# Turned squares go through HBM: one transfer out and four back in place of sixteen inside SBUF

## The chip, the cores and the metric

The kernel runs on one core of a Trainium2 chip. A core has five engines that run their own instruction queues side by side: TensorE (matmuls; PE in the profile, and PEld for its weight loads), VectorE (DVE), ScalarE (ACT), GpSimd (POOL) and SyncE (SP), which here only issues transfers. Sixteen DMA engines move data between HBM and the on-chip memory SBUF, which has 128 partitions; matmul results stand in PSUM. The metric is the device time of one execution in microseconds (us), the median of several runs.

## The reference

One decoder layer for 256 tokens of width 2048, in float32:

- `h = RMSNorm(x)`, `z = h @ w_in`, a projection to 7176 columns, split among the heads.
- Four mLSTM heads of 256 channels: `s = (q k^T)` weighted by an exponential of gates, then `s @ v`, divided by a stabilised sum, RMS-normalised per head, times the sigmoid of an output gate.
- Eight attention heads of 128 channels with normalised q and k and a cumulative log-forget bias in a causal softmax.
- `x = x + concat(heads) @ w_out`.
- `u = RMSNorm(x) @ w_up`, halves `a` and `g` of 5632 columns; `a` goes through a causal depthwise convolution of width 3; `x = x + (gelu(a) * g) @ w_down`.
- `x = x + sigmoid(RMSNorm(x) @ w_ple_gate) * (p @ w_ple_proj)`.

## The kernel before

**Matmuls in three products.** Every weight block of 128 x 1024 numbers is loaded by SP as `raw`; ScalarE writes its rounded copy `hi` and VectorE the rest `lo = raw - hi` (L273 and L275 in the first half, L1001 and L1003 in the second). The activations are split the same way. TensorE then adds three products: activation-hi by weight-hi, activation-hi by weight-lo, activation-lo by weight-hi (L304 to L306, L1292 to L1294, L1053 to L1055). A 512-wide matmul starts every 0.227 us; a block of 12 takes 2.72 us.

**Order of the work.** `run_stream` goes through the blocks of `w_in` and `w_out`, `run_units` through the units of `w_up`, `w_down` and the last gate. Loads run ahead by the free `raw` buffers, splits by three to six blocks (`AHEAD_SPLIT`, `PARTS`, `PARTS2`). Work beside the matmuls is hooked on: in the first half generators in `side`, two steps pulled per block; in the second half jobs hung on units by `with_after`, and put behind named splits by `between` (`tc.issue_after`). A planner then fixes each engine's queue before anything runs, from modelled times (`schedule_with_timeline_sim=True`), and adds the waits. On the chip each queue runs in that order.

**Mixed units.** Each group `up_group(q)` but the first carries four units that multiply two of its channel blocks with seven products in place of eight. They need sums of weight blocks on VectorE (`T`, L1325 to L1327) and are split from `xs`. `up_group(q)` has 16 or 18 units and takes 42.8 us; there are 11. Their weights are in `w_up`, then `down` runs twice over the columns of `w_down`, also with such mixed units.

**Turned squares.** Results come with tokens in the partitions; the next matmul wants channels in the partitions. Where TensorE does not transpose, this is done in two steps. `square` (L184, VectorE) transposes 32 x 32 blocks in place, each inside its 32 partitions. `move` then carries the blocks to the right 32 partitions: for each of four source partition groups `a` and four destination groups `b` one transfer from SBUF to SBUF, all issued by POOL (L190):

```
for a in range(4):
    for b in range(4):
        pool.dma_start(out=c[32 * b : 32 * b + 32, a::4], in_=y[32 * a : 32 * a + 32, :, b])
```

There are 25 moves. Four carry the pairs of q and k heads (`qk_squares`, from `qky` to `qkz`), four mLSTM q and k (`qk_group`, from `my` in the tile `spare` to `mqT` or `mk`), one the first two gated mLSTM heads (`mlstm_gate`, `hay` to `haz`), three the new x (`resid`, `x2y` to `x2z`), two x before the last gate (`x3_squares`): 512 KB each. The eleven of the up projection (`up_turn`, from `Y` to `EZ`) carry 1 MB each.

**Who reads them.** `column` takes 32 columns of each moved block, scales them into `hi` on ScalarE (L201) and `lo` on VectorE (L202); `columns` waits until seven blocks have been traced since the move (`since(7, ...)`). `fox_heads` copies q and k on ScalarE (L532), `mk_columns` mLSTM k (L593), and TensorE reads `mqT` directly through `feature` (L641, L644). In the up projection `up_act(q)` runs while group q + 1 is multiplied, from its ninth-last unit on: `first` copies half `a` on ScalarE (L901), four `conv` steps follow (L906, L909), and `last` applies GELU (L915), multiplies by half `g` on VectorE (L916) and splits the result (L140, L141). For some channel pairs `left_sums` then stores sums of it to HBM, also from POOL (L873).

**POOL's other work.** Broadcasts of gate rows (L515), reciprocal roots for the norms (L165), and these stores. They stand in one queue with the moves.

Of the kernel before, what the change touches and what calls it, by code (L numbers as in the profile page):

```python
# [49 lines left out]
def layer_kernel(  # L50
# [7 lines left out]
    act, dve, pe, pool = nc.scalar, nc.vector, nc.tensor, nc.gpsimd  # L58
# [7 lines left out]
    mp = mixers.enter_context(tc.tile_pool(name="mix", bufs=1))  # L66
    kp = ctx.enter_context(tc.tile_pool(name="kept", bufs=1, space=bass.MemoryType.DRAM))
# [7 lines left out]
    def f32(ap):  # L75
        return ap.bitcast(F32)
# [98 lines left out]

    def squares(name):

        return mp.tile([P, NT, 4, 128], F32, tag="sq", name=name)

    def square(y, t, k, src):  # L180

        n = src.shape[1] // P
        o = y[:, t, :, 32 * k : 32 * (k + n)].rearrange("p b (k j) -> p k b j", j=32)
        dve.transpose(o, src)  # L184

    def move(y, c):

        for a in range(4):
            for b in range(4):
                pool.dma_start(out=c[32 * b : 32 * b + 32, a::4], in_=y[32 * a : 32 * a + 32, :, b])  # L190

    def gather(y, name):
        c = mp.tile([P, NT * 4, 128], F32, tag="col", name=name)
        move(y, c)
        return c, done[0]

    def column(c, k, dst, gain):

        src = c[:, :, 32 * k : 32 * k + 32]
        hi, lo = (dst[:, o : o + 256].rearrange("p (a j) -> p a j", j=32) for o in (0, 256))  # L200
        act.activation(hi, src, AF.Copy, scale=gain)  # L201
        dve.scalar_tensor_tensor(out=lo, in0=src, scalar=gain, in1=f32(hi), op0=ALU.mult, op1=ALU.subtract)  # L202

    def columns(yz, dst, k0, gain):

# [137 lines left out]
    with mixers:  # L343
# [19 lines left out]
        my = spare[:, 1024:2048].rearrange("p (t b c) -> p t b c", t=NT, b=4)  # L363
        ssq1 = sm.tile([P, NT, 8], F32, name="ssq1")
        r1 = {}

# [152 lines left out]
        def fox_heads():  # L519
            zv = z["fv"]  # L520

            def gen(heads):
# [3 lines left out]
                for h in heads:  # L526
                    while h // 2 not in qkz or not since(7, qkz[h // 2][1]):
                        yield
                    w = qkz[h // 2][0].rearrange("p a (c h j) -> p h c a j", c=2, h=2)[:, h % 2]
                    qk = mp.tile([P, 512], F32, tag="qk", name="qk", bufs=2)  # L530
                    for c, g_ in ((0, g_fq), (1, g_fk)):
                        act.activation(qk[:, c * 256 : (c + 1) * 256].rearrange("p (a j) -> p a j", j=32),  # L532
                                       w[:, c], AF.Copy, scale=g_)
                    taken.add(h)
                    if h ^ 1 in taken and h // 2 + 1 < FH // 2:
# [46 lines left out]
            side.append(gen(range(1, FH, 2)))  # L582


        mqT = mp.tile([P, 2, NT * 4, P], F32, name="mqT")
        mkT = mp.tile([P, 8, S], F32, name="mkT")

        mk_in = set()
# [1 line left out]
        def mk_columns(grp, start):  # L590
            while not since(7, start):
                yield
            act.copy(mkT[:, 4 * grp : 4 * grp + 4].rearrange("p k (a j) -> p k a j", j=32),  # L593
                     z["mk"][:, grp].rearrange("p a (k j) -> p k a j", j=32))
            mk_in.add(grp)
            yield

        def qk_group(name, grp):
            def f(t, b):
                act.activation(mz[:, t], b, AF.Copy, scale=r1["t"][:, t : t + 1])  # L600
                square(my, t, 0, mz[:, t])
                if t < NT - 1:
                    return
                if name == "mq":
                    move(my, mqT[:, grp])
                    return
                if grp == 0:
                    z["mk"] = zbuf("mk").rearrange("p t c -> p (t c)")[:, 0:2048].rearrange("p (g a c) -> p g a c", g=2, c=P)
                move(my, z["mk"][:, grp])
                side.append(mk_columns(grp, done[0]))  # L610
            return f

        def feature(m, k, t0, t1):

            return m[:, k // 4, 4 * t0 : 4 * t1, 32 * (k % 4) : 32 * (k % 4) + 32]

        WT = {}

# [191 lines left out]
    with tc.tile_pool(name="ffn", bufs=1) as fp:  # L810
# [61 lines left out]
            sums_of(u, f, t)  # L872
            pool.dma_start(out=sums[SEVEN.index(p_)], in_=f32(t).rearrange("p i c -> p (i c)"))  # L873

        Z = EZ.rearrange("p t (a c) -> p (t a) c", c=256)
        a_ = Y[:, 0:BLK].rearrange("p (k s) -> p k s", k=4)
        c_ = Y[:, BLK : 2 * BLK].rearrange("p (k s) -> p k s", k=4)

        def runs(v):
            return v.rearrange("p a (k r) -> p k a r", r=32)  # L880

        def by_run(v):
            return v.rearrange("p k (a r) -> p k a r", r=32)

        def up_rows(t, n, b):

# [1 line left out]

        def up_turn(q):

            y = Y.rearrange("p (t b c) -> p t b c", t=NT, b=4)
            for t in range(NT):
                if q > 0:
                    dve.tensor_add(EZ[:, t], EZ[:, t], xs[:, 1, t * BLK : (t + 1) * BLK])
                square(y, t, 0, EZ[:, t])
            move(y, Z)

        def up_act(q):

            def first():  # L900
                act.copy(by_run(a_), runs(Z[:, :, 0:128]))  # L901
# [12 lines left out]
            def last():  # L914
                act.activation(c_, c_, AF.Gelu)  # L915
                dve.tensor_mul(by_run(c_), by_run(c_), runs(Z[:, :, 128:256]))  # L916
# [256 lines left out]
        def x3_squares(i):  # L1173
            def f(*_):
                if i == 0:
                    x3s["t"] = fp.tile([P, 2, 2, 1024], F32, tag="uB", name="x3s")
                y, z_ = x3s["t"][:, i, 0], x3s["t"][:, i, 1].rearrange("p (a c) -> p a c", c=P)
                y = y.rearrange("p (t b c) -> p t b c", t=NT, b=4)
# [280 lines left out]
```

## Time and profile before

| | us |
|---|---|
| median of 3 runs (1241.19 to 1241.99) | 1241.44 |
| the profiled execution | 1241.07 |
| its span, first to last instruction | 1239.1 |
| TensorE busy | 1232.5 |
| VectorE busy | 901.0 |
| ScalarE busy | 720.9 |
| POOL busy | 244.2 |

The granted TensorE clock is 1.00 throughout. DMA queues moved 276.35 MB, 223 GB/s on average; the queue of POOL's transfers (software_dynamic) 25.50 MB of it, in 7.2% of the time of 16 engines.

How to read the rows: a timeline row gives the start, the duration, engine, code line, operation, out<-in, and in brackets the idle time before and what ended it. `x9` means nine merged neighbours. A group row gives the busy total and the mean in ns. A waits row gives who waited for whom, the total, the number of times and the longest. A row of transfers gives engine, count, KB each and the median us from issue to landing. A row of a stretch gives for PE, PEld, DVE, ACT and POOL the busy time and the count, then the clock, the DMA engines' busy share and GB/s. Tile names are the program's; `hi`, `lo`, `w` are split weights (`w` the two extra buffers of the late part).

### The profile page before, as it was taken

The numbers are of one execution on the slowest core, as the hardware profiler recorded it, in microseconds if no ns is written. First come the engines' busy times: TensorE is split into PE (matmuls) and PEld (weight loads), VectorE is DVE, ScalarE is ACT, GpSimd is POOL, SyncE is SP. The second block draws the span as 40 slices with busy tenths as digits, with TensorE's granted clock in tenths as the row PEclk, the third lists the DMA queues.
The fourth block names the chain that finished last, engine by engine and source line by source line (L and its number), as shares of the span: only waits on it lengthen the run. The fifth ranks groups of instructions, "written<-read, shape, count | busy, mean of one in ns | idle before, by whom it ended". The sixth has DMA issues, their size and how long they took to land.

```text
span 1239.1 us, 16191 instructions
## 1 busy us (share of the span) xinstructions
PE 1232.5 (99%) x5638; PEld 1039.3 (84%) x5638; DVE 901.0 (73%) x1125; ACT 720.9 (58%) x1000; POOL 244.2 (20%) x457
## 2 busy tenths in 40 slices
PE   9999999999999999999999999999999999999998
PEld 7999988888888888888888888888888888888887
DVE  5455566665565665888888898888778998998653
ACT  7565455554554454766676576657645555566542
POOL 2001256513304202022202211220220000050000
PEclk9999999999999999999999999999999999999999
DMA  8766877766557797776877777676895996777560
GB/s 242 207 187 185 233 215 220 207 194 177 173 187 223 217 340 219 223 227 217 260 236 212 224 254 243 192 237 193 257 294 171 316 359 204 264 236 251 179 211 34
DMA packets 134370, 276.35 MB, mean 223 GB/s; under 512 B 15065, under 2 KB 30033, under 8 KB 134161
## 3 DMA queue, kind: packets, MB, share of 16 engines
q1 hardware_dynamic: 118864, 249.66, 64.3%
q0 software_dynamic: 15040, 25.50, 7.2%
q8 instruction: 44, 0.72, 0.2%
q14 instruction: 37, 0.30, 0.1%
q10 hardware_dynamic: 385, 0.16, 0.0%
HBM read 247.46 MB, written 8.93 MB: 207 GB/s over the span
## 4 chain that ended last, share of the span: by engine, by line
PE 99%; DMA 0%; SPq 0%; DVE 0%; ACT 0%; issue 0%; DVEq 0%
PE tg L304 13%; PE tg L305 13%; PE tg L306 13%; PE up L1292 12%; PE up L1294 12%; PE up L1293 12%; PE dnP L1054 1%; PE dnP L1055 1%; PE dnP L1053 1%; PE upP L1292 1%; PE upP L1294 1%; PE upP L1293 1%; PE dn(0, 1)_7885 L1055 1%; PE dn(0, 0)_7881 L1054 1%; PE dn(0, 1)_7885 L1054 1%; PE dn(1, 0)_7889 L1054 1%
## 5 line engine op out<-in xcount | busy, mean ns | idle before, releaser
L275 DVE TENSOR_TENSOR lo<-raw,hi 128x1024 fp32r<-128x1024 f32 (+3 forms) x153 | 177.7, 1162 | 154.8 <-ACT hi L273 154.4
L1294 PE MATMUL up<-hi,x2T 128*128 128x512 f32 x644 | 250.7, 389 | 0.0
L1293 PE MATMUL up<-lo,x2T 128*128 128x512 f32 x644 | 250.6, 389 | 0.0
L273 ACT CAST hi<-raw 128x1024 fp32r<-128x1024 f32 (+3 forms) x153 | 153.1, 1001 | 155.3 <-PE tg L306 122.7
L1292 PE MATMUL up<-hi,x2T 128*128 128x512 f32 x644 | 221.3, 389 | 0.0
L305 PE MATMUL tg<-lo,hT 128*128 128x512 f32 (+2 forms) x480 | 181.5, 379 | 0.0
L304 PE MATMUL tg<-hi,hT 128*128 128x512 f32 (+2 forms) x480 | 180.9, 382 | 0.0
L306 PE MATMUL tg<-hi,hT 128*128 128x512 f32 (+2 forms) x480 | 180.3, 377 | 0.0
L1003 DVE TENSOR_TENSOR lo<-raw,hi 128x1024 fp32r<-128x1024 f32 (+1 forms) x118 | 137.2, 1171 | 43.4 <-ACT hi L1001 42.8
L1001 ACT CAST hi<-raw 128x1024 fp32r<-128x1024 f32 (+1 forms) x118 | 118.8, 1014 | 81.6 <-PE up L1294 35.9
L1294 PEld LDWEIGHTS up<-hi,x2T 128*128 128x128 f32 x644 | 120.9, 188 | 25.1
L1293 PEld LDWEIGHTS up<-lo,x2T 128*128 128x128 f32 x644 | 120.9, 188 | 25.0
L1292 PEld LDWEIGHTS up<-hi,x2T 128*128 128x128 f32 x644 | 120.9, 188 | 25.0
L190 POOL DMA_DIRECT2D EZ<-Y x176 | 93.1, 536 | 122.7 <-DVE Y L184 52.1
L306 PEld LDWEIGHTS tg<-hi,hT 128*128 128x128 f32 x480 | 90.1, 188 | 12.5
L305 PEld LDWEIGHTS tg<-lo,hT 128*128 128x128 f32 x480 | 90.2, 188 | 11.7 <-DVE lo L275 0.3
L304 PEld LDWEIGHTS tg<-hi,hT 128*128 128x128 f32 x480 | 89.7, 188 | 11.7
L1001 ACT CAST hi<-xs 128x1024 fp32r<-128x1024 f32 (+1 forms) x43 | 40.8, 952 | 71.1 <-PE up L1294 50.0
L1003 DVE TENSOR_TENSOR lo<-xs,hi 128x1024 fp32r<-128x1024 f32 (+1 forms) x43 | 47.1, 1098 | 34.7 <-ACT hi L1001 34.7
L873 POOL DMA_DIRECT2D sums<-Sp x9 | 5.2, 575 | 272.3 <-DVE Sp L866 272.3
L1003 DVE TENSOR_TENSOR lo<-u36r,hi 128x1024 fp32r<-128x1024 f32 x36 | 43.6, 1215 | 11.8 <-ACT hi L1001 10.3
L1001 ACT CAST w<-raw 128x1024 fp32r<-128x1024 f32 x27 | 28.4, 1053 | 38.3 <-DVE raw L1102 27.1
(695 smaller groups left out, 2351.9 us busy)
## 6 DMA issues: line engine op xcount, KB each, us to landing
raw<-in_w_in_dram SPq DMA_DIRECT2D x71, 512.0 KB, 4.2
raw<-in_w_up_dram SPq DMA_DIRECT2D x68, 512.0 KB, 5.2
raw<-in_w_down_dram SPq DMA_DIRECT2D x43, 512.0 KB, 6.0
u36r<-in_w_up_dram SPq DMA_DIRECT2D x36, 512.0 KB, 5.0
raw<-in_w_in_dram SPq DMA_DIRECT2D x40, 432.0 KB, 3.8
raw<-in_w_out_dram SPq DMA_DIRECT2D x32, 512.0 KB, 4.7
u32r<-in_w_up_dram SPq DMA_DIRECT2D x31, 512.0 KB, 5.2
EZ<-Y POOLq DMA_DIRECT2D x176, 64.0 KB, 4.6
```

Source lines behind the costliest of these rows:

```text
L190: pool.dma_start(out=c[32 * b : 32 * b + 32, a::4], in_=y[32 * a : 32 * a + 32, :, b])
L273: act.copy(hi, raw[:, :w])
L275: dve.tensor_sub(lo, raw[:, :w], f32(hi))
L304: pe.matmul(o, ah, hi[:, i, :], start=first, stop=False)
L305: pe.matmul(o, ah, lo[:, i, :], start=False, stop=False)
L306: pe.matmul(o, al, hi[:, i, :], start=False, stop=last)
L1001: act.copy(hi, raw)
L1003: dve.tensor_sub(lo, raw, f32(hi))
L1054: pe.matmul(o, ah, lo, start=False, stop=False)
L1292: pe.matmul(o, ah, hi, start=start, stop=False)
L1293: pe.matmul(o, ah, lo, start=False, stop=False)
L1294: pe.matmul(o, al, hi, start=False, stop=stop)
```

## The change

`move` now writes the whole square tile to a scratch tile in HBM (`hop`, two buffers of each width) in one transfer, and reads it back in four, one for each destination group of 32 partitions; all five are issued by POOL. The reads wait for the write. To make the runs contiguous (1 KB or 2 KB for a read, 4 KB or 8 KB for the write) the order of dimensions inside a square changes: destination block first, then token half `t`, and in the moved tile source group `a` before `t`. So every reader walks `t` and `a` in another order. Two VectorE operations are cut in halves by `t`: `lo` in `column`, and the product with half `g` in `last`.

```diff
     def squares(name):
-        return mp.tile([P, NT, 4, 128], F32, tag="sq", name=name)
+        return mp.tile([P, 4, NT, 128], F32, tag="sq", name=name)

     def square(y, t, k, src):
...
-        o = y[:, t, :, 32 * k : 32 * (k + n)].rearrange("p b (k j) -> p k b j", j=32)
+        o = y[:, :, t, 32 * k : 32 * (k + n)].rearrange("p b (k j) -> p k b j", j=32)
         dve.transpose(o, src)

     def move(y, c):
-        for a in range(4):
-            for b in range(4):
-                pool.dma_start(out=c[32 * b : 32 * b + 32, a::4], in_=y[32 * a : 32 * a + 32, :, b])
+        w = y.shape[3]
+        hop = kp.tile([P, 4, NT, w], F32, tag=f"hop{w}", name=f"hop{w}", bufs=2)
+        pool.dma_start(out=hop, in_=y)
+        v = hop.rearrange("(a p) b t c -> p a b (t c)", a=4)
+        for b in range(4):
+            pool.dma_start(out=c[32 * b : 32 * b + 32].rearrange("p a t c -> p a (t c)"), in_=v[:, :, b])
+
+    def tokens(v):
+        return v.rearrange("p a t j -> p t a j")
...
     def column(c, k, dst, gain):
-        src = c[:, :, 32 * k : 32 * k + 32]
-        hi, lo = (dst[:, o : o + 256].rearrange("p (a j) -> p a j", j=32) for o in (0, 256))
+        src = tokens(c[:, :, :, 32 * k : 32 * k + 32])
+        hi, lo = (dst[:, o : o + 256].rearrange("p (t a j) -> p t a j", t=NT, j=32) for o in (0, 256))
         act.activation(hi, src, AF.Copy, scale=gain)
-        dve.scalar_tensor_tensor(out=lo, in0=src, scalar=gain, in1=f32(hi), op0=ALU.mult, op1=ALU.subtract)
+        for t in range(NT):
+            dve.scalar_tensor_tensor(out=lo[:, t], in0=src[:, t], scalar=gain, in1=f32(hi[:, t]),
+                                     op0=ALU.mult, op1=ALU.subtract)
...
         def feature(m, k, t0, t1):
-            return m[:, k // 4, 4 * t0 : 4 * t1, 32 * (k % 4) : 32 * (k % 4) + 32]
+            return tokens(m[:, k // 4, :, t0:t1, 32 * (k % 4) : 32 * (k % 4) + 32])
...
             def first():
-                act.copy(by_run(a_), runs(Z[:, :, 0:128]))
+                act.copy(by_run(a_), runs(Z[..., 0:128]))
...
                 act.activation(c_, c_, AF.Gelu)
-                dve.tensor_mul(by_run(c_), by_run(c_), runs(Z[:, :, 128:256]))
+                for t in range(NT):
+                    v = by_run(c_)[:, :, t]
+                    dve.tensor_mul(v, v, runs(Z[..., 128:256])[:, :, t])
```

The rest of the diff adapts the shapes of `my`, `mqT`, `z["mk"]`, `Z`, `Y` and the x3 tiles, and the readers in `fox_heads` and `mk_columns`, to this order.

More of the change, by code (lines that the diff above doesn't have):

```diff
@@ L362, in layer_kernel @@
         mz = spare[:, 0:1024].rearrange("p (t c) -> p t c", t=NT)
-        my = spare[:, 1024:2048].rearrange("p (t b c) -> p t b c", t=NT, b=4)
+        my = spare[:, 1024:2048].rearrange("p (b t c) -> p b t c", t=NT, b=4)
         ssq1 = sm.tile([P, NT, 8], F32, name="ssq1")
@@ L582, in fox_heads @@
             side.append(gen(range(1, FH, 2)))
-        mqT = mp.tile([P, 2, NT * 4, P], F32, name="mqT")
+        mqT = mp.tile([P, 2, 4, NT, P], F32, name="mqT")
         mkT = mp.tile([P, 8, S], F32, name="mkT")
@@ L592, in mk_columns @@
                 yield
-            act.copy(mkT[:, 4 * grp : 4 * grp + 4].rearrange("p k (a j) -> p k a j", j=32),
-                     z["mk"][:, grp].rearrange("p a (k j) -> p k a j", j=32))
+            act.copy(mkT[:, 4 * grp : 4 * grp + 4].rearrange("p k (t a j) -> p k t a j", t=NT, j=32),
+                     z["mk"][:, grp].rearrange("p a t (k j) -> p k t a j", j=32))
             mk_in.add(grp)
@@ L607, in f @@
                 if grp == 0:
-                    z["mk"] = zbuf("mk").rearrange("p t c -> p (t c)")[:, 0:2048].rearrange("p (g a c) -> p g a c", g=2, c=P)
+                    z["mk"] = zbuf("mk").rearrange("p t c -> p (t c)")[:, 0:2048].rearrange("p (g a t c) -> p g a t c", g=2, t=NT, c=P)
                 move(my, z["mk"][:, grp])
@@ L873, in left_sums @@
             pool.dma_start(out=sums[SEVEN.index(p_)], in_=f32(t).rearrange("p i c -> p (i c)"))
-        Z = EZ.rearrange("p t (a c) -> p (t a) c", c=256)
+        Z = EZ.rearrange("p t c -> p (t c)").rearrange("p (a t c) -> p a t c", t=NT, c=256)
         a_ = Y[:, 0:BLK].rearrange("p (k s) -> p k s", k=4)
@@ L879, in runs @@
         def runs(v):
-            return v.rearrange("p a (k r) -> p k a r", r=32)
+            return v.rearrange("p a t (k r) -> p k t a r", r=32)
         def by_run(v):
-            return v.rearrange("p k (a r) -> p k a r", r=32)
+            return v.rearrange("p k (t a r) -> p k t a r", t=NT, r=32)
         def up_rows(t, n, b):
@@ L889, in up_turn @@
         def up_turn(q):
-            y = Y.rearrange("p (t b c) -> p t b c", t=NT, b=4)
+            y = Y.rearrange("p (b t c) -> p b t c", t=NT, b=4)
             for t in range(NT):
@@ L1176, in f @@
                     x3s["t"] = fp.tile([P, 2, 2, 1024], F32, tag="uB", name="x3s")
-                y, z_ = x3s["t"][:, i, 0], x3s["t"][:, i, 1].rearrange("p (a c) -> p a c", c=P)
-                y = y.rearrange("p (t b c) -> p t b c", t=NT, b=4)
+                y, z_ = x3s["t"][:, i, 0], x3s["t"][:, i, 1].rearrange("p (a t c) -> p a t c", t=NT, c=P)
+                y = y.rearrange("p (b t c) -> p b t c", t=NT, b=4)
                 for t in range(NT):
```

6 lines of the change are left out of this document (3 added, 3 removed).

## The prediction

> **What bounds the kernel now.** I read the page's busy times and chain first, then the waits of the two TensorE rows, then a timeline of each hand-over that the change touches.
>
> ```profile
> span 1239.1 us, 16191 instructions
> PE 1232.5 (99%) x5638; PEld 1039.3 (84%) x5638; DVE 901.0 (73%) x1125; ACT 720.9 (58%) x1000; POOL 244.2 (20%) x457
> PE 99%; DMA 0%; SPq 0%; DVE 0%; ACT 0%; issue 0%; DVEq 0%
> ```
>
> The chain that ended last is TensorE throughout. A busy TensorE could still be a waiting one, so the waits decide.
>
> ```profile
> PE warm L93 <- DVE ones L89: 1.1, 1, 1.1
> PE xT L152 <- DMA xs<-in_x_dram: 1.0, 1, 1.0
> PEld tg L305 <- DVE lo L275: 0.3, 1, 0.3
> ```
>
> These are waits of the first microseconds; none names a turned square. So TensorE is the bound, nothing the moves could release is on its path, and the change can matter only by making TensorE wait. What protects it is the lead: ScalarE's `hi` and VectorE's `lo` of a weight block are ready some microseconds before TensorE reads them. The n-th split belongs to the n-th unit of the written order, so I paired them over the kernel (1,798 `lo` products, as the code has). After the 30 us of start-up the smallest leads are these. First, the mixed units of the up projection, in the second and the eighth of its eleven groups (`up_group` 1 and 7; 1 to 7 all lie between 1.74 and 1.76 us).
>
> ```profile
> 494.18 1.23 DVE L1003 TENSOR_TENSOR lo<-xs,hi 128x1024 fp32r<-128x1024 f32 x1 [1.20 <-ACT hi L1001]
> 497.15 0.39 PE L1293 MATMUL up<-lo,S_up 128*128 128x512 f32 x1
> 751.22 1.22 DVE L1003 TENSOR_TENSOR lo<-xs,hi 128x1024 fp32r<-128x1024 f32 x1 [1.19 <-ACT hi L1001]
> 754.19 0.39 PE L1293 MATMUL up<-lo,S_up 128*128 128x512 f32 x1
> ```
>
> VectorE ends at 495.41 and TensorE reads at 497.15: 1.74 us. Second, the start of the down projection, where loads are late.
>
> ```profile
> 905.00:932.00 27.00, 27.00 (x121) 22.36 (x120) 15.20 (x15) 9.85 (x13) 9.09 (x17) 1.00 0.90 281
> 932.45 1.05 ACT L1001 CAST hi<-raw 128x1024 fp32r<-128x1024 f32 x1 [8.94 <-DMA raw<-in_w_down_dram]
> 933.53 1.23 DVE L1003 TENSOR_TENSOR lo<-raw,hi 128x1024 fp32r<-128x1024 f32 x1 [8.77 <-ACT hi L1001]
> 937.79 0.39 PE L1054 MATMUL dn(0, 0)_7881<-lo,uA 128*128 128x512 f32 x1
> 974.47 1.22 DVE L1003 TENSOR_TENSOR w<-raw,w 128x1024 fp32r<-128x1024 f32 x1
> 978.14 0.39 PE L1054 MATMUL dn(1, 0)_7889<-lo,uC 128*128 128x512 f32 x1
> ```
>
> From 905 to 932 us the DMA engines are 90% busy, ScalarE waits 8.94 us for a load, and the lead is 937.79 - 934.76 = 3.03 us; at 978.14 it is 2.45.
>
> **The move itself.** There are 25 moves: 4 of query-key pairs, 4 of mLSTM q and k, 1 of the gated heads, 3 of x2, 11 of the up projection, 2 of x3. Each loses 16 POOL transfers and gets 5. I take the up projection's, twice as large as the others.
>
> ```profile
> 526.25 4.73 POOL L190 DMA_DIRECT2D EZ<-Y  x9 [36.77 <-ACT hi L1001]
> 535.67 2.24 POOL L190 DMA_DIRECT2D EZ<-Y  x4 [1.64 <-DMA EZ<-Y]
> 546.42 1.03 ACT L901 COPY Y<-EZ 128x1024 f32<-128x1024 f32 x1
> 548.43 1.23 DVE L1003 TENSOR_TENSOR lo<-u36r,hi 128x1024 fp32r<-128x1024 f32 x1 [2.18 <-ACT hi L1001]
> 554.27 0.39 PE L1293 MATMUL up<-lo,x2T 128*128 128x512 f32 x1
> EZ<-Y POOLq DMA_DIRECT2D x176, 64.0 KB, 4.6
> sums<-Sp POOLq DMA_DIRECT2D x9, 512.0 KB, 4.8
> kept_x<-xs SPq DMA_DIRECT2D x1, 2048.0 KB, 9.3
> xs<-in_w_up_dram SPq DMA_DIRECT2D x20, 256.0 KB, 5.4
> rowF<-keptF POOLq DMA_DIRECT2D x8, 128.0 KB, 4.2
> L873 POOL DMA_DIRECT2D sums<-Sp x9 | 5.2, 575 | 272.3 <-DVE Sp L866 272.3
> L190 POOL DMA_DIRECT2D EZ<-Y x176 | 93.1, 536 | 122.7 <-DVE Y L184 52.1 <-ACT hi L1001 36.8 <-DMA EZ<-Y 25.8
> ```
>
> Now: first issue 526.25, last issued by 537.91, landed 4.6 us after its issue at 537.4, so about 542: 15.8 us. The reader, ScalarE's first copy, starts at 546.42, 20.2 us after the first issue. After: one 1 MB transfer out. Between 4.8 us (512 KB to HBM) and 9.3 us (2 MB) the straight line gives 6.3. Then POOL, which now waits for that landing, issues four (575 ns each is the row for a large one, 2.3 us), and the last 256 KB lands 5.4 us after its issue at +1.7: 6.3 + 1.7 + 5.4 = 13.4 us. Upper end, with 9.3 for the write and 10.4 for a read (the slowest load group of the crowded stretch, quoted below): 21.4. Even that is 1.2 us behind the old reader, whose neighbour on VectorE ends at 549.66 for a read at 554.27, a lead of 4.61. So nothing reaches TensorE at either end; I take 13.4, since the 512 KB row is on the same queue and of the same kind. For the 512 KB moves: 4.8 + 1.7 + 4.2 = 10.7 us. The least covered of them is the gated heads':
>
> ```profile
> 328.27 5.46 POOL L190 DMA_DIRECT2D haz<-hay  x10 [0.19 <-issue]
> 337.15 2.11 POOL L190 DMA_DIRECT2D haz<-hay  x4 [1.91 <-DMA haz<-hay]
> 345.63 1.71 ACT L201 ACTIVATE catT<-haz,vT 128x256 fp32r<-128x256 f32 x4
> ```
>
> 17.4 us from first issue to reader, against 10.7 after. What queues behind the new wait on POOL are the row broadcasts, the reciprocal roots and the stores of sums. POOL held 16 x 536 ns = 8.6 us and more of issuing, and now holds 0.6 + 6.3 + 2.3 = 9.2 for a large move and 7.7 for a small one: no worse than the 11.7 us of the row above. Cost 0, covered by those spans. The buffers `Y`, `my` and `sq` are free once the write out has landed, which is earlier than now.
>
> [...]
>
> **VectorE and ScalarE.** `lo` of a column becomes two halves, and so does the product with the gate.
>
> ```profile
> L202 DVE SCALAR_TENSOR_TENSOR x3T<-x3s,vT,x3T 128x256 fp32r<-128x256 f32 x8 | 3.3, 476 | 0.0
> L861 DVE TENSOR_TENSOR Sf<-Y 128x128 f32<-128x128 f32 x9 | 2.6, 284 | 0.0
> L916 DVE TENSOR_TENSOR Y<-Y,EZ 128x1024 f32<-128x1024 f32 x11 | 13.4, 1219 | 1.2 <-ACT Y L915 1.1
> L1222 DVE TENSOR_TENSOR Y<-Y,tg 128x512 f32<-128x512 f32 x7 | 4.7, 682 | 16.6 <-ACT Y L1221 16.6
> L593 ACT COPY mkT<-mk 128x1024 f32<-128x1024 f32 x2 | 2.1, 1052 | 0.0
> L901 ACT COPY Y<-EZ 128x1024 f32<-128x1024 f32 x11 | 11.4, 1035 | 0.0
> ```
>
> 24 columns (12 of x2, 4, 8 of x3) grow by 2 x 284 - 476 = 92 ns, 11 gate products by 2 x 682 - 1219 = 145 ns: 2.2 + 1.6 = 3.8 us of VectorE spread over 900, at most 0.15 us against a lead of 2.45 where it is nearest. On the path: 0. Reordered reads and transposes keep 32-element runs; ScalarE's copies with such runs already take 1035 and 1052 ns per 1024 columns, like its other casts, so 0; no row shows another stride between the runs, and I bound that at 5% of such an operation either way, under 0.1 us.
>
> **The bytes.** This is the one term with teeth.
>
> ```profile
> GB/s 369 307 253 328 307 198 273 376 382 396 382 410 416 403 423 416 410 417 423 328 294 232 341 212 212 260 280 335 253 253 266 301 273 150 171 198 164 68 82 41
> xs<-in_w_down_dram SPq DMA_DIRECT2D x3, 512.0 KB, 10.4
> ```
>
> That is 908 to 932 us in 0.6 us slices, with the last up-projection move from 916.5 on. The move carries 1.05 MB now and 2.1 MB after, half of it through HBM. If all the extra 1.05 MB stood ahead of the late load at 281 GB/s, that would land 3.7 us later: 0.7 us beyond the 3.03, or 1.3 beyond the 2.45 if VectorE, dense until 975, makes up nothing. Lower end: 0, since the rate itself falls from some 410 to 250 GB/s when the old transfers start, and a write out of all 128 partitions may not do that. The read-back begins only after the write has landed, some 7 us or more after 916.5, so most of it comes after the load; half ahead is 1.85 us, under both leads. I take 0.
>
> [...]
>
> Sum: 0 on the profiled execution's 1241.07 us (span 1239.1 and 1.97 around it). The median of the runs is 0.37 above it, so the forecast is 1241.4. What goes away, 25 x 11 POOL issues, was never on the path.
>
> **Rivals.**
> - *The order shifts (slower).* Each engine's order is made beforehand from modelled times, and a hop through HBM is modelled otherwise. In groups 1 to 7 the lead is 1.74 us. If the copies, convolution steps or gate work of the group before fall ahead of the mixed units, one 1.22 us operation costs nothing, two (2.44) cost 0.7 us in each of 7 groups: 4.9 us, 1246.3; three cost 13.4, 1254.8. It decides from 2.1 us of shifted work, where 7 x 0.36 is 0.2%. For it: VectorE has no other slack there. Against: the readers are tied behind named splits, and sit 20 us after the move already.
> - *The hop is late (slower).* From 20.2 + 4.6 = 24.8 us for a large move each further microsecond costs about 10 us over the groups; at 26 us it would be 1253. No row comes near.
> - *The loads of the down projection arrive over 4.9 us later (slower).* That costs over 2.5 us: 1244 to 1246, and needs more than the whole extra megabyte ahead of them.
> - *Faster.* TensorE's idle time is 1239.1 - 1232.5 = 6.6 us, of start and end; no wait in it is a move's. At most some tenths, 1240.5.
> - *It doesn't do what it says:* the hop, waiting, holds POOL as long as 16 issues did. This gives 1241.4 too.
>
> **How the numbers follow.** About 0.2%, 2.5 us, is what tells a change of this kernel from none. Unchanged 0.66 (its own range 1240.6 to 1243.9), faster 0.03, order shift 0.14, late hop 0.06, late loads 0.06, other slower causes 0.05. Up to 1247.5 the range takes in the late loads and the two-operation shift. Left out are three operations, the late hop, half of the others and the faster case, together just under 0.2.
>
> **What would show it.** Right: POOL's busy time falls by some 140 us from 244.2 (25 x (16 x 536 - 5 x 575) ns), five transfers per move with the reads 5 to 7 us behind the write, TensorE's waits unchanged, the copy at L901's place not waiting for DMA. Wrong: a row of waits of TensorE on VectorE's `lo` at the mixed units, near 938, or on a copy whose releaser is the read-back.

## The result, and the profile after

The changed kernel takes 1262.88 us (median of 4 runs, 1261.95 to 1263.66) where the kernel before takes 1241.72 on the same chip: a ratio of 1.017, 95% interval 1.0152 to 1.0188. It is slower by 21 us, and the forecast of 1241.4, with its range to 1247.5, was wrong.

The head of the page after:

```profile
span 1261.3 us, 15869 instructions
PE 1242.6 (99%) x5638; PEld 1041.5 (83%) x5638; DVE 907.3 (72%) x1160; ACT 718.8 (57%) x1000; POOL 100.2 (8%) x182
PE 61%; DMA 4%; issue 3%; POOL 1%; DVE 1%; ACT 0%; DVEq 0%; POOLq 0%; ACTq 0%
```

POOL's busy time fell by 144 us, and the chain that ended last, TensorE throughout before, now holds transfers, POOL and issue time. TensorE's four longest waits (columns: us in total, times, longest):

```profile
PE up L1303 <- ACT hi L1012: 2.4, 1, 2.4
PE ob L584 <- ACT PT L580: 2.0, 1, 2.0
PE dn(0, 0)_8526 L1064 <- ACT w L1012: 1.7, 1, 1.7
PE dnP L1064 <- ACT w L1012: 1.5, 1, 1.5
```

None of these names a moved square. Three are for weight splits and one for `PT`, a copy in the attention heads. ScalarE makes all of them, and they come late because it stood elsewhere. Five rows of its own waits, of the same kernel:

```profile
ACT hi L282 <- DMA raw<-in_w_in_dram: 61.3, 28, 5.6
ACT x2T L208 <- DMA x2z<-hop: 11.1, 3, 5.1
ACT x3T L208 <- DMA x3s<-hop: 10.4, 2, 8.0
ACT mkT L602 <- DMA mk<-hop: 9.7, 2, 5.6
ACT Y L910 <- DMA EZ<-hop: 6.9, 2, 6.5
```

Four of the five rows are readers that now wait for a read-back through HBM. The first is weight loads of `w_in`, for which ScalarE waited 14.8 us in all before; for those of `w_out` it waits 20.2 us where it waited 5.5.

Both kernels have 5638 matmuls. Compared one by one in order of their start, in the profiled executions, those of the changed kernel fall behind by 3.9 us up to 315 us (the heads), by 8.5 between 404 and 469 us (x2) and by 9.7 between 1115 and 1136 us (x3). The clearest place is x3. First the kernel before, then the changed one, in timeline rows:

```profile
1083.94 4.21 POOL L190 DMA_DIRECT2D x3s<-x3s  x8 [154.74 <-PE dn(0, 1)_8733 L1055]
1101.40 1.70 ACT L201 ACTIVATE x3T<-x3s,vT 128x256 fp32r<-128x256 f32 x4
```

```profile
1096.26 0.56 POOL L190 DMA_DIRECT2D hop<-x3s  x1 [158.14 <-DVE x3s L184]
1104.09 4.38 POOL L193 DMA_DIRECT2D x3s<-hop  x8 [6.09 <-issue]
1114.56 1.71 ACT L208 ACTIVATE x3T<-x3s,vT 128x256 fp32r<-128x256 f32 x4 [8.01 <-DMA x3s<-hop]
1117.26 0.50 PE L1064 MATMUL dn(0, 0)_8526<-w,uT 128*128 128x512 f32 x1 [1.70 <-ACT w L1012]
1119.56 1.70 ACT L208 ACTIVATE x3T<-x3s,vT 128x256 fp32r<-128x256 f32 x4 [2.35 <-DMA x3s<-hop]
```

Before, ScalarE came to the first reader 17.5 us after the move began and did not wait. After, it came to it 10.3 us after (1114.56 - 8.01 - 1096.26), and stood 8.01 us. The move itself is not done in the 10.7 us of the prediction but in 18.3. The weight casts behind the reader are what TensorE waits for at 1117.26.

Why ScalarE came so early is in the written order of its queue. Counted in weight casts that stand ahead of each reader:

| reader | before | after |
|---|---|---|
| q and k (`fox_heads`) | 67, 68, 74, 87, 98 | 67, 68, 71, 71, 77, 84 |
| mLSTM k (`mk_columns`) | 104, 110 | 89, 96 |
| gated heads, into `catT` | 125 | 122 |
| x2 | 140, 149, 157 | 137, 145, 153 |
| x3 | 458, 470 | 454, 455 |

(The q and k readers split into another number of groups.) But for the first two of q and k, every reader of a 512 KB move on ScalarE stands earlier, though the code that calls them is the same. In the up projection nine of the eleven readers stand one cast earlier. The rows of landing (queue, count, KB each, median us from issue to landing) say how long the new transfers take:

```profile
hop<-Y POOLq DMA_DIRECT2D x11, 1024.0 KB, 6.3
EZ<-hop POOLq DMA_DIRECT2D x44, 256.0 KB, 5.3
x2z<-hop POOLq DMA_DIRECT2D x12, 128.0 KB, 7.3
hop<-x3s POOLq DMA_DIRECT2D x2, 512.0 KB, 7.8
x3s<-hop POOLq DMA_DIRECT2D x8, 128.0 KB, 9.2
```

Theory A, then: the hop makes the planner place the readers earlier in ScalarE's queue than their data lands, and the weight casts queued behind them come late. Rival B: the transfers, by their bytes or the time that they hold queues, delay the weight loads wherever the readers stand. That the planner's model of the hop is too short is inferred from the places; no run looks into the model.

### The profile page after: what moved, and what is told of

Same layout as the page of the kernel before. It is cut to its first block, busy times and chain, and to the rows that moved or that the text cites. A ratio compares the mean times of both kernels' runs of the same rounds, so it can differ in the third digit from the quotient of the medians.

```text
span 1261.3 us, 15869 instructions
## 1 busy us (share of the span) xinstructions
PE 1242.6 (99%) x5638; PEld 1041.5 (83%) x5638; DVE 907.3 (72%) x1160; ACT 718.8 (57%) x1000; POOL 100.2 (8%) x182
## 4 chain that ended last, share of the span: by engine, by line
PE 61%; DMA 4%; issue 3%; POOL 1%; DVE 1%; ACT 0%; DVEq 0%; POOLq 0%; ACTq 0%
PE up L1304 11%; PE up L1305 11%; PE up L1303 11%; PE tg L313 2%; PE tg L314 2%; PE tg L315 2%; DMA raw<-in_w_up_dram 1%; PE dnP L1065 1%; PE dnP L1066 1%; PE dnP L1064 1%; DMA x3s<-hop 1%; DMA hop<-x2y 1%; PE upP L1303 1%; PE upP L1305 1%; PE upP L1304 1%
## 5 line engine op out<-in xcount | busy, mean ns | idle before, releaser
L314 PE MATMUL tg<-lo,catT 128*128 128x512 f32 x128 | 49.9, 390 | 0.8 <-DVE lo L284 0.8
L1012 ACT CAST hi<-u36r 128x1024 fp32r<-128x1024 f32 x36 | 37.7, 1053 | 22.3 <-PE up L1305 22.3
L313 PE MATMUL tg<-hi,catT 128*128 128x512 f32 x128 | 50.1, 391 | 0.3 <-ACT hi L282 0.3
```

The source lines that it names most:

```text
L313: pe.matmul(o, ah, hi[:, i, :], start=first, stop=False)
L314: pe.matmul(o, ah, lo[:, i, :], start=False, stop=False)
L1012: act.copy(hi, raw)
```

## The experiments

### One part alone

All of these keep the new layout and the halved VectorE operations. The first has the old transfers everywhere, the others take the hop for some moves only.

```diff
     def move(y, c, hops=False):
-        (always the hop)
+        if hops:
+            (the hop)
+        else:
+            for a in range(4):
+                for b in range(4):
+                    pool.dma_start(out=c[32 * b : 32 * b + 32, a], in_=y[32 * a : 32 * a + 32, b])
```

> The sixteen transfers from SBUF to SBUF are put back; the new order of dimensions, the halved VectorE operations and the changed readers stay. Theory A (the written order of the readers): 1241 to 1243 us, ScalarE's readers stand behind 140, 149, 157, 458 and 470 weight casts as before, and none of them waits for DMA. Theory B (bytes through HBM): also 1241 to 1243. Theory C (the layout and the halved operations cost): about 1262.

Measured: 1240.40 us, ratio 0.9993 (0.9984 to 1.0003). Layout and halves cost nothing.

> Only the eleven 1 MB moves of the up projection go through HBM; the fourteen 512 KB moves are sixteen transfers again. Theory A: 1241 to 1244 us, because the readers of the 512 KB moves are back in their old places, and the up projection's reader had room (one wait of 6.5 us, covered by the lead). Theory B: the up projection carries 11.5 of the 18.9 MB, so some 60% of the 21 us stay: about 1254.

Measured: 1241.75 us, 1.0005 (0.9995 to 1.0014). The eleven 1 MB moves, three fifths of the bytes, cost nothing that can be told.

> Only the two moves of x3 go through HBM. Their readers stand behind 454 and 455 weight casts, as in the changed kernel, against 458 and 470 before. Theory A (ScalarE, in its written order, stands before a read-back that has not landed, and the casts behind it starve TensorE): one stall near 1100 to 1115 with matmuls at a lower clock after it, +8 to +10 us, 1249 to 1251. Theory B (bytes through HBM): 1 of 18.9 MB, so +1 us, 1242.

Measured: 1248.56 us, 1.0058 (1.0043 to 1.0073).

> Only the three moves of x2 go through HBM, their readers behind 137, 145 and 153 casts in place of 140, 149 and 157. Theory A: ScalarE waits 2 to 5 us at each, and the third delays the loads at the start of the up projection; +5 to +8 us, 1246 to 1249. Theory B: 1.6 of 18.9 MB, +2 us, 1243.

Measured: 1247.96 us, 1.0051 (1.0036 to 1.0066). Both lie near theory A's 1249 to 1251 and 1246 to 1249 us and well over theory B's 1242 and 1243.

> Only the nine moves of the heads go through HBM. The readers of q, k stand up to 14 casts earlier than before, those of mLSTM k 14 and 15. Theory A: the stalls near 210 and 268 stay, +3 to +5 us, 1244 to 1246. Theory B: 4.7 of 18.9 MB, +5 us, 1246. This run sizes the part and does not tell the two apart.

Measured: 1248.84 us, 1.0055 (1.0038 to 1.0071). This is more than the 1244 to 1246 us that either theory expected. In this kernel TensorE's waits have one large row:

```profile
PE ob L592 <- ACT PT L588: 5.7, 1, 5.7
```

ScalarE copies `PT`. Its rows ahead of that copy, and the late load in the chain that ended last (start, us, what):

```profile
208.16 1.05 ACT L290 CAST hi<-raw 128x1024 fp32r<-128x1024 f32 x1 [5.85 <-DMA raw<-in_w_in_dram]
214.46 1.04 ACT L290 CAST hi<-raw 128x1024 fp32r<-128x1024 f32 x1 [5.24 <-DMA raw<-in_w_in_dram]
215.41 0.85 ACT L588 COPY PT<-pt 128x384 f32<-128x384 f32 x2
202.55 11.80 DMA raw<-in_w_in_dram
```

What stops ScalarE here is not a read-back but weight loads, one of which took 11.8 us. That is what rival B describes; whether it happens wherever the readers stand is asked by `heads_held` below.

Against the kernel before on the same chip, 1240.65 us, or 1240.91 for the up projection's run, the parts are 7.9, 7.3, 8.2 and 0.8 us, together 24 beside 21 for all. So 14 moves of 512 KB carry the loss, a third of it in two moves of x3.

### Only the traffic

The old transfers carry the data. The write to the hop and four reads from it go on as well, into a second scratch tile that nobody reads.

```diff
         pool.dma_start(out=hop, in_=y)
+        (the sixteen transfers from y to c)
         v = hop.rearrange("(a p) b t c -> p a b (t c)", a=4)
         for b in range(4):
-            pool.dma_start(out=c[32 * b : 32 * b + 32].rearrange("p a t c -> p a (t c)"), in_=v[:, :, b])
+            pool.dma_start(out=sink[32 * b : 32 * b + 32].rearrange("p a t c -> p a (t c)"), in_=v[:, :, b])
```

> The sixteen transfers carry the data, and beside them every move makes the hop's traffic with nobody waiting for it: one write to HBM and four reads of it, which go on to a second scratch tile in HBM. Theory A: 1241 to 1246 us, since the readers stand where they stood or later. Theory B: more bytes than in the changed kernel, so 1262 us or more.

Measured: 1253.10 us, 1.0096 (1.0079 to 1.0112), in the range of neither theory. The readers stood at 141, 149 and 157 and at 459 and 471, within one cast of before. Of the 11.4 us by which the matmuls fall behind, some 10 are lost in one place, the gated heads, where the move begins at 351 us and not at 328:

```profile
PE hap L727 <- DVE mv L724: 6.9, 1, 6.9
362.10 0.72 POOL L165 TENSOR_TENSOR rh<-rs_v,neghalf 128x2 f32<-128x2 f32 x1
362.86 0.88 DVE L724 SCALAR_TENSOR_TENSOR mv<-mv,rh,mo 128x256 f32<-128x256 f32 x2 [2.95 <-POOL rh L165]
```

A reciprocal root (`rh`) stands in POOL's queue behind the sixteen transfers, VectorE waits for it and TensorE for VectorE. ScalarE's own wait for this move, 5.2 us, ends later, at 364.64. Here POOL issues 21 transfers per move and no read-back is waited for, so this loss goes through POOL's queue and not through a reader on ScalarE; the stalls of x2 and x3 are absent, with all their traffic there. It doesn't separate A from B for the heads.

### Readers held back

The readers are tied behind a named weight cast, so that they stand where they stood before; the transfers stay in HBM. First for x2, mLSTM k and x3 with all hops, later more of them, then for x3 and the heads alone.

```diff
+    def held(job):
+        if rush:
+            job()
+        else:
+            with tc.issue_after(last["hi"]):
+                job()
...
-            return lambda *_: [column(x3s[k // 4], k % 4, get_x3T()[:, k], g_ple[:, k : k + 1]) for k in ks]
+            return lambda *_: [held(lambda: column(x3s[k // 4], k % 4, get_x3T()[:, k], g_ple[:, k : k + 1]))
+                               for k in ks]
```

> All moves go through HBM as in the changed kernel, but the readers of x2, x3 and of mLSTM k are held in the written order: two blocks more are counted before them and each is put behind the weight cast traced last. They stand behind 140, 148, 154, 458 and 464 casts in place of 137, 145, 153, 454 and 455. Theory A: the 9 us around 1115 to 1130 and the stall near 414 go, those near 210 and 437 to 464 may stay: 1243 to 1251 us. Theory B: the bytes are the same, so 1258 to 1263.

Measured: 1254.07 us, 1.0088 (1.0056 to 1.0121), with runs from 1244.54 to 1255.87. The stalls near 414 and 1115 us are gone; a TensorE wait of 6.2 us stays in the heads, whose q and k readers were not held (`ob` waits for `PT`), and one of 4.2 after the third x2 move (`up` waits for `hi`).

`held_more` also holds the q and k readers (`since(10, ...)` in place of 7, places 69, 79, 89, 99) and turns the third x2 block with TensorE, as the code does for the fourth (`if c < 2` in place of `if c < 3`). So 24 moves hop.

> The held readers of the earlier run, and in addition the readers of the attention's q and k held (behind 69, 79, 89 and 99 casts, near the 67, 74, 87 and 98 before), and the third x2 move taken out: its columns are transposed on TensorE like those of the fourth quarter. 24 moves still go through HBM. Theory A: no stall near 210, 440 or 1115 is left, 1241 to 1244 us, the extra transposes costing TensorE about 0.9. Theory B: 18.4 of 18.9 MB still hop, 1258 or more.

Measured: 1245.17 us, 1.0032 (1.0022 to 1.0042), 4.5 us above the kernel before and over what theory A expected. The profiled execution, 1242.79, is among the fastest of its runs and has no wait of TensorE over 0.4 us past the start, so it doesn't show where the rest is lost. The 0.9 us expected for the extra transposes was an estimate, and no run has them alone.

> Only the two moves of x3 go through HBM; their readers on ScalarE (the copies of x3T) are held back in the written order to where they stood before, behind 458 and 464 of the weight casts in place of 454 and 455. Theory A (the place of the reader in ScalarE's order is the cost, since the read-backs land later than that place): the 8 us of TensorE's wait at 1103 to 1107 us goes and the time is 1241 to 1243 us. Rival B (the transfers themselves, their bytes or their queue, slow the weight loads whatever the reader's place): about 1249 us, as with the readers early.

Measured: 1240.98 us, 0.9997 (0.9988 to 1.0007). The x3 moves go through HBM and cost nothing. In the timeline:

```profile
1083.59 0.55 POOL L194 DMA_DIRECT2D hop<-x3s  x1 [153.30 <-DVE x3s L187]
1090.74 2.21 POOL L197 DMA_DIRECT2D x3s<-hop  x4 [5.43 <-DMA hop<-x3s]
1093.35 2.17 POOL L197 DMA_DIRECT2D x3s<-hop  x4 [0.39 <-issue]
1101.33 1.70 ACT L216 ACTIVATE x3T<-x3s,vT 128x256 fp32r<-128x256 f32 x4
1112.65 1.70 ACT L216 ACTIVATE x3T<-x3s,vT 128x256 fp32r<-128x256 f32 x4
```

The first reader stands behind 458 casts again, comes 17.7 us after the first write was issued, and waits for nothing; the second stands behind 464.

The converse, with no transfer through HBM: the x3 readers, hung at channel block 27 of `down` in place of 31 and 35, are put ahead of the next weight cast, behind 453 of them.

```diff
-                    31: x3_columns(0, 1, 2, 3), 35: x3_columns(4, 5, 6, 7)}
+                    27: lambda *a: [f(*a) for f in (x3_squares(1), x3_columns(0, 1, 2, 3), x3_columns(4, 5, 6, 7))]}
...
         def part(hi, lo, raw):
-            act.copy(hi, raw)
+            if early:
+                with tc.issue_after(early.pop()):
+                    act.copy(hi, raw)
+            else:
+                act.copy(hi, raw)
```

> The converse: no transfer goes through HBM, all 25 moves are sixteen transfers inside SBUF, but the eight readers of x3 on ScalarE are forced ahead of later weight casts, behind 453 of them in place of 458 and 464 to 470. Theory A (a reader that stands in ScalarE's order before its data has landed is the cost, whatever the transport): the last of the 32 old transfers was issued 22 us after the first, so ScalarE stands until some 1110 us where with the hop it was free at 1106; with that 4 us more of waiting than the 7.9 us of the two hopped moves of x3, 1250 to 1257 us, with TensorE waiting between 1102 and 1112 us. Rival B (the transfers through HBM, not the place, cost the time): 1241 us as before.

Measured: 1254.13 us, 1.0104 (1.0089 to 1.0119). Its two reader rows and TensorE's wait:

```profile
1101.86 1.70 ACT L207 ACTIVATE x3T<-x3s,vT 128x256 fp32r<-128x256 f32 x4 [6.89 <-DMA x3s<-x3s]
1107.97 1.70 ACT L207 ACTIVATE x3T<-x3s,vT 128x256 fp32r<-128x256 f32 x4 [4.41 <-DMA x3s<-x3s]
```

```profile
PE dn(0, 0)_8756 L1069 <- ACT hi L1015: 11.4, 1, 11.4
```

So for x3 it is settled both ways: hop and late place cost nothing, old transfers and early place cost 13.5 us. In these two runs the place is the cost, not the transport.

> Only the nine moves of the heads go through HBM; the readers of the q and k moves are held behind 69, 79, 89 and 99 weight casts and the later mk reader behind 105, in place of 67 to 84 and 96. Theory A (place in ScalarE's order): the wait of 5.8 us at 210 us goes, 1241 to 1244 us. Rival B (the queue is at 45% of the DMA engines between 195 and 212 us in place of 18%, so the weight tiles come late whatever the order): the wait stays near 210 us, 1246 to 1249 us. In between, say 1244 to 1246 us with a smaller wait at the same place, both have a share.

Measured: 1243.93 us, 1.0021 (1.0008 to 1.0034). The wait at 210 us is gone, and 5.5 of the 8.2 us with it; some 2.7 remain. But this is not the case of x3, since no read-back stopped ScalarE ahead of that wait. Its waits for `w_in`, in the kernel before, with the heads' hops, and with the same and readers held (with the up projection's hops alone they are 15.1 us):

```profile
ACT hi L273 <- DMA raw<-in_w_in_dram: 14.8, 10, 2.9
```

```profile
ACT hi L290 <- DMA raw<-in_w_in_dram: 58.5, 30, 5.8
```

```profile
ACT hi L298 <- DMA raw<-in_w_in_dram: 53.4, 32, 6.9
```

In sum ScalarE waits nearly as long for these loads with the readers held. At the place of the stall it doesn't: loads of 512 KB that are issued between 185 and 215 us land after a median of 5.1 us before, 9.7 with the heads' hops and 4.5 with the readers held. Holding the readers also changed the order of POOL's transfers: between 197 and 209 us two row loads stand among them with the readers early and none with the readers held. So for the heads the run shows that the written orders decide whether loads and moves collide; it does not show that a reader ahead of its data was the cost. The 2.7 us that remain may be B as well: the longest of these waits, 6.9 us up to 181 us, is for a load issued right behind two writes to the hop, and it took 7.1 us. No run isolates that.

The DMA engines between 195 and 212 us, before and in the changed kernel, where the loads are late too (the last two columns are the DMA share and GB/s):

```profile
195.00:212.00 17.00, 17.00 (x76) 14.08 (x75) 11.56 (x19) 6.87 (x9) 8.88 (x18) 1.00 0.72 207
```

```profile
195.00:212.00 17.00, 16.01 (x74) 12.93 (x72) 10.47 (x23) 8.04 (x18) 6.76 (x12) 1.00 0.93 252
```

### The third move of x2

> Only the three moves of x2 go through HBM; their readers are held behind 141, 149 and 155 weight casts in place of 137, 145 and 153 (before: 140, 149, 157). Theory A: the two first are where they were and cost nothing; the third is still two casts early, so the stalls near 432 and 453 us shrink but need not go: 1241 to 1245 us. Rival B (landing of the read-backs and the bytes): as with the readers early, about 1248 us, with ScalarE or TensorE late near 453 us just the same.

Edit: `since(10, start)` for x2 and `held` around its columns; places 141, 149 and 155. Measured: 1249.83 us, 1.0064 (1.0042 to 1.0085), no better than with the readers early. ScalarE now waits for a weight load, 9.35 us, where TensorE waits 3.8:

```profile
452.07 1.04 ACT L1025 CAST hi<-raw 128x1024 fp32r<-128x1024 f32 x1 [9.35 <-DMA raw<-in_w_up_dram]
```

Another order had changed too. SyncE writes x, 2 MB, to `kept_x` before the up projection. Before, that write stood ahead of the loads of `u32r`, `u36r` and `u40r`; where the third x2 move hops it stands behind those five, right ahead of the load that is late. The next runs take this apart: two hops with the third move old (`HOPS = ('x2z0', 'x2z1')`), the write put back, the write put late with old transfers.

```diff
-        with_after(us[6], move_x(True))
+        move_x(True)()
+        last["kept"] = traced()
...
+                    if j in (6, 7, 8, 9, 10, 11):
+                        with tc.issue_after(last["kept"]):
+                            load()
```

> Only the first and the second move of x2 go through HBM, readers early (behind 137 and 145 weight casts); the third is sixteen transfers, its reader behind 156, and the write of kept_x stands where it did before in SyncE's order. If the third move alone makes the loss: 1241 to 1243 us. If the early readers of the two first cost it: 1246 to 1248 us.

Measured: 1242.42 us, 1.0008 (0.9999 to 1.0018). So the third move makes most of the loss of x2; the 1.2 us that stay are not told from nothing.

> As x2_held (three moves of x2 through HBM, readers behind 141, 149 and 155 casts), with the 2 MB write of kept_x put back ahead of the loads of u32r, u36r and u40r in SyncE's order. Theory C (the write moved behind five loads stands, by its size, right ahead of the loads that TensorE then waits for near 453 us): 1241 to 1243 us, no wait near 453 us. Rival (the third reader, still two casts early, or the read-backs themselves): 1246 to 1250 us as x2_held.

Measured: 1245.61 us, 1.0025 (1.0011 to 1.0039), 4.4 us above the kernel before, where `x2_held` is 9.2 above it; a TensorE wait of 2.6 us stays where none was expected, up to 454.5 us, behind a load that ScalarE waits 7.9 us for.

> The converse: all moves are the old sixteen transfers with all readers at their old places, and only the 2 MB write of kept_x is put behind the next six weight loads in SyncE's order. Theory C: TensorE waits 2 to 6 us near 450 to 460 us, 1244 to 1248 us. Rival (the order of the write does not matter): 1240 to 1242 us.

Measured: 1241.77 us, 1.0002 (0.9993 to 1.0011). The late write alone, from which 3 to 7 us were expected, costs nothing.

Last, both orders with the old transfers. The first four weight casts of the up projection are tied behind the third x2 reader, as `part` above does for x3; in the second run `kept_x` is late as well.

> The converse for x2: all moves are the old sixteen transfers; only the readers of the third x2 move are put ahead of the first four weight casts of the up projection, behind 153 casts in place of 157; the write of kept_x stays ahead of the loads of u32r. Theory A (the reader's place): ScalarE stands until some 431 to 433 us, the four casts and with them the free load buffers come late, TensorE waits near 450 us: 1243 to 1247 us. Rival (only a hop in that place costs): 1241 us.

Measured: 1248.53 us, 1.0055 (1.0038 to 1.0071). But this is not the clean converse that it was meant as. In its timeline the reader doesn't wait for its data; it stands behind other late work, the sums of squares of the new x:

```profile
433.01 0.63 ACT L158 ACTIVATE junk<-xs 128x512 f32<-128x512 f32 x1 [8.70 <-DVE xs L786]
436.43 1.71 ACT L205 ACTIVATE x2T<-x2z,vT 128x256 fp32r<-128x256 f32 x4
438.03 1.04 ACT L1013 CAST hi<-raw 128x1024 fp32r<-128x1024 f32 x1
```

It shows that four weight casts put behind late work cost 7 us here, though what that work waits for is no move.

> As the run with the third x2 reader early and the old transfers, and the write of kept_x also behind the loads of u32r, u36r and u40r: the two written orders that the hop of x2 brings, without the hop. Theory (the orders together are the loss): 1246 to 1249 us, as the x2 hop has. If the read-backs through HBM have a part of their own: 1243 to 1245 us. If neither order matters: 1241 us.

Measured: 1253.40 us, 1.0096 (1.0081 to 1.0111), 4.9 us more than without the late write, and more than was expected of it. In two pairs of runs the write in that place costs some 5 us (4.8 and 4.9), and alone nothing. Here the casts have held the load buffers: SyncE issues no load from 425.2 to 439.2 us and then eight in 5 us, ahead of the write. That this is the difference is read from the traces and not tested. What of the third move's loss stays with the write put back, 4.4 us, isn't settled: its reader is still two casts early, and no run put it at 157 with the hop.

### All of it together

All 25 moves hop, these readers (but not that of the gated heads) are held and `kept_x` is put back.

> All 25 moves through HBM as in the changed kernel, the readers of q, k, mLSTM k, x2 and x3 held and kept_x put back. If the two orders (readers on ScalarE, kept_x on SyncE) are the whole loss: 1241 to 1244 us. If the transfers cost something by themselves: above 1245 us. Faster than before by over 2.5 us is expected by neither.

Measured: 1247.19 us, 1.0042 (1.0030 to 1.0053). Of the 21 us, 15 come back with nothing but orders changed. The rest lies above the 1245 us that were set as the sign of a cost of the transfers themselves, but doesn't prove it, since the third x2 reader (155 casts, before 157) and that of the gated heads (121, before 125) are still early. In the profiled execution, 5.8 us behind that of the kernel before, 2.5 us are lost in the first 15 us, ahead of any move, 2.3 between 174 and 198 us and 0.6 at 450 to 462 us. ScalarE's waits for `w_in` stay at 63.3 us in this kernel. No kernel here is faster than the one before by more than its interval.

## Why the prediction was wrong

**What bounds the kernel, and what decides.** Right: TensorE was the bound with no wait, and the change could only matter by making it wait.

**The step that failed** is the costing of the 512 KB moves: "Cost 0, covered by those spans". The spans, 17.4 us for the gated heads and 20.2 for the up projection, were read off the kernel before and taken as fixed. They are no property of the program but the planner's placement of the reader, and the planner moved it with the transfer that it reads: behind 454 weight casts and not 458 at x3, 10.3 us and not 17.5 behind the start of the move. `x3_held` and `sixteen_early` show for x3 that this is the cost, and `all_held_kept` gives back 15 of the 21 us by orders alone. For the heads the orders are shown to cost two thirds, but the wait that reached TensorE in `hop_only_heads` was for late weight loads and not for a read-back; for the third x2 move 4.4 us stay open. Nor was the gated heads' span the least covered: the second q and k move, first issued at 168.67 us, had its reader at 184.23, 15.6 us.

**The size of the move** failed as well. "4.8 + 1.7 + 4.2 = 10.7 us" took the reads from the `rowF` row of 4.2; the landings were 5.9 us for `mqT`, 6.4 to 7.3 for q and k, mLSTM k, the gated heads and x2, and 9.2 for x3, whose write took 7.8 and not 4.8, so the move at x3 took 18.3. With its reader in the old place that is covered (`x3_held`); with moved ones it set the wait.

**The large moves** cost nothing, as forecast, but with less to spare. The medians, 6.3 us for the write and 5.3 for a read, stand beside the 6.3 and 5.4 that were worked out. Yet ten of the moves took 14.1 to 16.1 us and not 13.4, because the reads started some 0.6 us after the write had landed and the last of four landed mostly later than the median. The readers came 15.8 us after the start in most and not 20.1. The last move, from 927 us on beside the loads of `w_down`, took 25.1 us, past the 24.8 from which the prediction saw a cost; ScalarE waited 6.5 us for it, and TensorE did not wait.

**VectorE and the layout.** Right that they are hidden (`sixteen_new_layout`), though half a `lo` takes 345 ns and not 284, and VectorE's busy time grew by 6.3 us and not 3.8. The 5% that the prediction allowed ScalarE's copies for the other stride between the runs was its author's guess, worked out from no row; the copy of half `a` (`Y<-EZ`) takes 1046 ns in the mean where it took 1035, and that of mLSTM k 1049 where it took 1052.

**The bytes** were looked for at 908 to 932 us, where TensorE lost nothing. The last large move began at 927.15 us: up to 935.35, while its write was under way, the DMA engines moved 420 GB/s, and 305 and 227 in the two stretches of 8 us behind it, with the reads. Where they were not looked for, between 195 and 212 us, the DMA share rose from 0.72 to 0.93 and `w_in` came late: with the heads' hops a load took 11.8 us and TensorE waited behind it. There the term of 0 was wrong. How much of the heads' 8.2 us are the transfers and how much the orders that make them collide is not separated; 2.7 stay with the readers held.

**The rivals.** "The order shifts" was the right mechanism at the wrong place: it was sought in the up projection's mixed units, where TensorE's lead is least, and priced by VectorE's work there. The argument against it, that the readers "are tied behind named splits", holds to within one cast for the up projection and not for the heads, x2 and x3, whose readers are only hung on a block count or a unit. The late hop was named for the large moves and came true for the small ones, x3 above all.

**What would show it.** POOL fell by 144 us where 140 was forecast. The releaser named as the sign of failure, a read-back, is there, on ScalarE; at x3 TensorE's wait shows only the cast behind it, and at 210 us in the heads the work behind a late weight load.

## What to carry to other kernels

Where a planner fixes each engine's order beforehand, a changed transfer also moves everything that reads it: compare the written orders of the engines before costing anything at zero. The lead of a reader in the old profile says what the old order allowed, not what the new one will: at x3 17.5 us before and 10.3 after. A reader put into an in-order queue ahead of its data stops unrelated work behind it (at x3 ScalarE stood 8.01 us, and TensorE 1.70 for a cast behind the reader), and tying it behind a named instruction gave back all of it for x3, two thirds for the heads and nothing for x2. Before blaming the reader, look at what the engine stood for: in the heads it was a weight load.

## What was not expected of the hardware

In the changed kernel TensorE ran on at a granted clock of 0.52 after some of its waits, in the stretches of 2.7 and 5.4 us shown below. After waits of 1.70, 1.10 and 1.46 us within 7 us, the matmuls from 1124.67 to 1129.43 start 0.43 us apart and not 0.227, and at 461.6, after one wait of 2.4 us, the same. The wait of 2.0 us near 213 us didn't bring it: the granted clock between 205 and 225 us is 1.00. The timeline of TensorE at x3, changed kernel:

```profile
1115.17 0.39 PE L1066 MATMUL dnP<-hi,uT 128*128 128x512 f32 x1
...
1119.09 0.50 PE L1065 MATMUL dn(0, 0)_8526<-w,uT 128*128 128x512 f32 x1 [1.10 <-DVE w L1014]
...
1122.25 1.22 PE L1064 MATMUL dnP<-w,S 128*128 128x512 f32 x2 [1.46 <-ACT w L1012]
1124.08 0.79 PE L1065 MATMUL dnP<-w,S 128*128 128x512 f32 x1 [0.61 <-DVE w L1014]
1124.67 0.63 PE L1066 MATMUL dnP<-w,S 128*128 128x512 f32 x1
...
1129.43 0.57 PE L1066 MATMUL dnP<-hi,S 128*128 128x512 f32 x1
1129.83 0.39 PE L1064 MATMUL dn(1, 0)_8534<-hi,uT 128*128 128x512 f32 x1
```

The stretches of the same kernel by engine (PE, PEld, DVE, ACT, POOL, then the granted clock, the DMA share and GB/s):

```profile
1092.00:1134.00 42.00, 37.13 (x144) 28.42 (x144) 34.08 (x52) 20.45 (x28) 5.50 (x10) 0.88 0.72 216
461.60:464.30 2.70, 2.70 (x8) 2.07 (x7) 2.70 (x3) 0.99 (x2) 0.00 (x0) 0.52 0.62 179
1124.60:1130.00 5.40, 5.40 (x14) 3.85 (x13) 5.37 (x7) 3.46 (x4) 0.00 (x0) 0.52 0.61 191
```

At x3, 22 matmuls between 1115.17 and 1129.83 took 14.7 us in place of 5.0. The four waits there, 1.70, 1.10, 1.46 and 0.61, are 4.9 of the lost 9.7. Steps from one matmul to the next that hold no wait lose 3.3, of it 3.0 from 1119.73 us on, with steps of 0.40 to 0.59 us; the other 1.5 stand beside the waits and are not separated. A stall doesn't simply cost twice its wait: in `sixteen_early` one of 11.4 us cost 13.5. One wait of 2.4 us was followed by the 0.52 and one of 2.0 us was not; what decides between them no run shows.
